# Merging the elementwise work of RWKV chunk steps over pairs and directions, with partition changes counted in the schedule

## The chip, the cores and the metric

The kernel runs on one core of a Trainium2 chip. The metric is the device time of one execution in microseconds (us): 3136.03 us, the median of 3 runs between 3131.77 and 3136.59. The profile is of a separate execution that took 3133.72 us; its span on the core is 3131.9 us. All numbers of the trace are from that one execution.

## What is computed

Two layers of a mixer over 640 tokens (128 context tokens, 512 latent ones) of width 2048. Every layer normalises and modulates its input, projects it with `w_in` to 7056 columns, runs three branches (gated linear attention with 6 heads, a chunked gMLP with 4 groups, bidirectional RWKV-7 with 12 heads), multiplies each by its gate and projects the result back with `w_out`. All matrix products of the projections are made in three parts of fp32r (a high and a low half of each factor). The change touches the RWKV branch, whose recurrence is, per head and direction,

```python
def step(s, inp):
    r_t, w_t, k_t, v_t, a_t, b_t = inp
    sa = jnp.einsum('bhvk,bhk->bhv', s, a_t)
    s = (s * w_t[:, :, None, :] + sa[..., None] * b_t[:, :, None, :]
         + v_t[..., None] * k_t[:, :, None, :])
    return s, jnp.einsum('bhvk,bhk->bhv', s, r_t)
```

The kernel runs it in chunks of 64 tokens: within a chunk everything is matrix products, and between chunks a 64x64 state per head and direction is handed on. With the state `s0`, the chunk's decay `p` per channel and the chunk's own contribution `Y`, both kernels compute the next state: before as `Y*p + s0*p`, after as `(Y + s0)*p`.

## The kernel before, in words

**The order is planned at build time.** Every operation is recorded by `rec` (line 134) and priced by `price` (line 215), and `run` (line 300) plays the program with one clock per engine. Each engine takes, of what is ready, the operation with the lowest priority number; the number is the place in the recording, less a boost for weights and for the RWKV chain. TensorE (`choose_pe`, line 363) prefers to go on with matrix products that use the whole array and collects small ones into groups. The order that comes out is fixed in the program: on the chip each engine takes its instructions in this order and waits for whichever is next. All instructions are issued from line 462, so the trace gives them that line, and they are told apart by their tiles. On VectorE an operation costs 0.066 us plus 0.00104 us per element (plus 0.062 us for a per-partition scalar); an operation that starts at another partition than the one before it costs nothing more. An engine's choice is made at line 402 for ScalarE and line 408 for the others.

**The RWKV branch** (`rwkv_quad`, line 895) works on a quad: two pairs of heads (`j`), both directions (`d`), five chunks. The two heads of a pair (`q`) lie in partitions 0 to 63 and 64 to 127. There are 12 quads (3 of each of 2 windows in 2 layers), one after the other, since they share the tiles `gb`, `ag`, `ken` and `svu`. A quad has a preparation (decays, the chunk matrices `ag`, `bk`, `gb`, and a 32x32 inversion on VectorE; from line 906 up to the steps) and then five chunk steps (the loop `for k in range(5)` from line 1075). A step is a chain:

1. ScalarE scales the eight states into `s0p` (`S.activation`, 64x64 each).
2. TensorE makes `X` and the first half of `Y` from `ag` and `svu`; VectorE copies `X` to `xs`.
3. TensorE adds `gb` times `xs`; VectorE copies the result back into `svu`, one copy for each direction and head (4 copies, 64x128).
4. TensorE adds the products with `ken` and `gb` to `Y`.
5. VectorE makes the next state, one `scalar_tensor_tensor` for each pair, direction and head (8 of 64x64), into `svu`, into `scar` (the state carried to the next window) or into `so` (the output state).

In the second window one direction hands no state on after the third step, and the other none after the fifth, so 432 of the 480 states (12 quads, 5 steps, 8 states) are made. The whole RWKV chain is boosted over everything but the weights. Between the chain's groups TensorE runs projections (`pz`), whose weights are split by ScalarE (`whi`) and VectorE (`wlo`), the other two branches and the modulation of the next layer (`mod_slow`, line 667; gangs of eight 128x32 products of 256 columns, priced at 0.111 us each). After the last quad `rwkv_end` (line 1194) finishes the branch and `out_proj` (line 1447) follows, which needs all branches.

Of the kernel before, what the change touches and what calls it, by code (L numbers as in the profile page):

```python
# [7 lines left out]
F32 = mybir.dt.float32  # L8
# [23 lines left out]


BOOST = 100000
RSTEP = 1
GANG = True
NRAW, NHI, NLO, N6 = 5,3,3,6
# [34 lines left out]

class _Op:
    __slots__ = ("idx", "eng", "fn", "args", "kw", "cost", "tail", "mode", "work", "lock", "succ", "npred", "ready", "prio",
                 "tiles", "first", "start", "end", "tab", "alts", "gang")


class Scheduler:
# [55 lines left out]
    def rec(self, eng, fn, args, kw):  # L134
        o = _Op()
        o.idx, o.eng, o.fn, o.args, o.kw = len(self.ops), eng, fn, args, kw
        o.succ, o.npred, o.ready, o.start, o.end = [], 0, 0.0, None, None
        o.prio = o.idx - self.boost
        wr, rd = [], []
        for i, a in enumerate(args):  # L140
            if hasattr(a, "tensor"):
                (wr if i == 0 else rd).append(a)
        for k, a in kw.items():
            if hasattr(a, "tensor"):
                (wr if k in ("out", "accum_out") else rd).append(a)
        self.price(o, eng, fn, wr, rd, kw)
        o.alts = None
        preds = {}
        names = set()
        rr = [r for r in map(self.region, rd) if r]  # L150
        ww = [r for r in map(self.region, wr) if r]
        for n, p0, p1, m in rr:
            names.add(n)
            for q0, q1, x, w in self.W.get(n, ()):
                if q0 < p1 and p0 < q1 and x & m:
                    preds[w] = 1
            if n in self.psum:
                for q0, q1, x, w in self.R.get(n, ()):
                    if self.ops[w].eng != eng:
                        preds[w] = 1  # L160
        for n, p0, p1, m in ww:
            names.add(n)
            for L, kind in ((self.W, 1), (self.R, 2)):
                keep = []
                for e in L.get(n, ()):
                    q0, q1, x, w = e
                    if q0 < p1 and p0 < q1 and x & m:
                        preds[w] = max(preds.get(w, 0), kind) if preds.get(w) != 1 else 1
                        if p0 <= q0 and q1 <= p1 and not (x & ~m):
                            continue  # L170
                    keep.append(e)
                L[n] = keep
        for n, p0, p1, m in rr:
            self.R.setdefault(n, []).append((p0, p1, m, o.idx))
        for n, p0, p1, m in ww:
            self.W.setdefault(n, []).append((p0, p1, m, o.idx))
        for n in names:
            preds.setdefault(self.head.setdefault(n, o.idx), 3)
        preds.pop(o.idx, None)
        o.gang = self.gang if eng == "PE" else None  # L180
        if o.gang is not None:
            for w in list(preds):
                if self.ops[w].gang is o.gang:
                    del preds[w]
            o.gang.append(o)
        for w, kind in preds.items():
            self.ops[w].succ.append((o.idx, kind))
        o.npred = len(preds)
        o.tiles = tuple(names)
        o.first = []  # L190
        for n in names:
            if n not in self.users:
                self.users[n] = 0
                t = self.tag[n]
                if t is not None:
                    self.seen.setdefault(t, []).append(n)
                    o.first.append(n)
            self.users[n] += 1
        self.ops.append(o)
        return o  # L200
# [14 lines left out]
    def price(self, o, eng, fn, wr, rd, kw):  # L215
# [9 lines left out]
        if eng == "PE":  # L225
            o.tail = 0.29
            if fn == "transpose":
                o.cost, o.work = 0.11, 0.053
                return
            l, r = kw["lhsT"], kw["rhs"]  # L230
            K, M, N = int(l.shape[0]), free(l), free(r)
            fast = l.dtype == F32R
            s = N / (2400 if fast else 600)
            o.work = s * K * M / 16384
            if (K == 128 or K * M == 0) and (M == 128 or (fast and M == 16)):
                o.cost = max(s + 0.0145, 0.107) if fast else max(s + 0.02, 0.15)
                return
            o.mode = f"{int(fast)} {K} {M}"
            if fast:
                o.cost = s + 0.0145  # L240
            elif M <= 32:
                o.cost = 0.03 if K <= 32 else 0.111 * N / 256
            elif M == 64:
                o.cost = (0.056 if K == 128 else 0.05) * max(N, 64) / 64
            else:
                o.cost = 0.55 if K == 16 else 0.206 * max(N, 100) / 128
            return
# [52 lines left out]
    def run(self):  # L300
# [11 lines left out]
        rel = {}  # L312
        order, dma, table, sw, mode = [], 0.0, None, 0, "full"
        window, work, fast = 0, 0.0, True
        left = dict(self.users)
        self.turns = 0

# [62 lines left out]
        while True:  # L380
# [15 lines left out]
            if e == "PE" and mode != "full" and all(ops[x[1]].mode == "full" for x in a):  # L396

                near = [x for x in f if x[0] < s + LINGER and ops[x[1]].mode != "full"]
                if near:
                    t[e] = min(near)[0]  # L400
                    continue
            if e == "ACT":

                i = take(a, min(range(len(a)), key=lambda j: (a[j][0] + (TABW if ops[a[j][1]].tab not in (None, table) else 0))))
            elif e == "PE":
                i = choose_pe(a, s)
            else:
                i = heapq.heappop(a)[1]
            o = ops[i]
            for n, o in enumerate(o.gang or [o]):  # L410
# [12 lines left out]
                elif o.tab is not None and o.tab != table:  # L423
                    x = 1.3
                    table = o.tab
                    sw += 1
                if o.lock:
                    s = free_at(e, True) if t[e] >= s else max(s, free_at(e, True))
                    locked[e] = s + c
# [64 lines left out]
def tile_hybrid(ctx: ExitStack, tc: tile.TileContext, I, O, layers=DEPTH, pairs=6, gpairs=3, cms=4, dbg=None):  # L494
# [71 lines left out]
    csp = cst.tile([128, KT, 32], F32, name="csp")  # L566
    modt = [cst.tile([128, 48, 2], F32, name=f"modt{l}") for l in range(layers)]
    amul = cst.tile([128, KT, 2], F32, name="amul")
    scar = [[cst.tile([128, 64], F32, name=f"scar{j}{d}") for d in range(2)] for j in range(2)]

    xr_d = dr.tile([NT, D], F32, name="xr_d")
    gate_d = [dr.tile([2, D], F32, name=f"gate_d{l}") for l in range(layers)]
# [318 lines left out]
    def product(out, a, b):  # L891
        f = dict(out=out, in0=a, in1=b, op=ALU.mult)
        V.tensor_tensor(**f)

    def rwkv_quad(l, P, wp, sts):

        ps2 = (2 * P, 2 * P + 1)
# [159 lines left out]
        for j, p in enumerate(ps2):  # L1057
            for d in range(2):
                for k, kind in start[d].items():
# [10 lines left out]
                            S.copy(out=svu[hq[q], j, d, q, pos(d, k), :], in_=ps[hq[q], 0:64])  # L1070
                    else:
                        for q in range(2):
                            S.copy(out=svu[hq[q], j, d, q, pos(d, k), :], in_=scar[j][d][hq[q], :])
        four = [(d, j, q) for d in range(2) for j in range(2) for q in range(2)]
        for k in range(5):
            X, Y = (PL().rearrange("p (a j d t) -> p a j d t", j=2, d=2, t=64) for _ in range(2))
            goes = [end[d].get(k, "next") for d in range(2)]
            s0p = ts2.tile([128, 2, 2, 64], F32, tag="s0p", name="s0p")
            sc = lambda d, j, q: p5[hq[q], 10 * j + 5 * d + pos(d, k):10 * j + 5 * d + pos(d, k) + 1]
            for d, j, q in four:  # L1080
                if goes[d]:
                    S.activation(out=s0p[hq[q], j, d], in_=svu[hq[q], j, d, q, pos(d, k), :], func=AF.Copy, scale=sc(d, j, q))
            with together():
                for d, j, q in four:
                    mm(X[hq[q], 0, j, d], ags[d][:, j, q, pos(d, k), 0:64], svu[:, j, d, q, pos(d, k), :], start=(d == 0 and j == 0))
# [4 lines left out]
            with together():  # L1090
                for d, j, q in four:
                    mm(X[hq[q], 1, j, d], gb[hq[q], j, d, pos(d, k), 0:64], xs[hq[q], j, d], start=False)
            for d in range(2):
                for q in range(2):
                    V.tensor_copy(out=svu[hq[q], :, d, q, pos(d, k), :], in_=X[hq[q], 1, :, d])
            with together():
                for d, j, q in four:
                    if goes[d]:
                        mm(Y[hq[q], 0, j, d], kens[d][:, j, q, pos(d, k), :], svu[:, j, d, q, pos(d, k), :], start=False)
                for d, j, q in four:  # L1100
                    mm(Y[hq[q], 1, j, d], gb[hq[q], j, d, pos(d, k), 64:128], svu[hq[q], j, d, q, pos(d, k), :], start=False)
            for j, p in enumerate(ps2):
                for d in range(2):
                    if not goes[d]:
                        continue
                    so = TS() if goes[d] == "out" else None
                    for q in range(2):
                        dst = svu[hq[q], j, d, q, pos(d, k + 1), :] if goes[d] == "next" else scar[j][d][hq[q], :] if goes[d] == "carry" else so[hq[q], :]
                        V.scalar_tensor_tensor(out=dst, in0=Y[hq[q], 0, j, d], scalar=sc(d, j, q), in1=s0p[hq[q], j, d], op0=ALU.mult, op1=ALU.add)
                    if so is not None:  # L1110
                        ps = PL()
                        for q in range(2):
                            mm(ps[hq[q], 0:64], so[hq[q], :], ident[hq[q], hq[q]])
                        s2 = TS()
                        S.copy(out=s2, in_=ps[:, 0:64])
                        Q.dma_start(out=O["new_rwkv"][0, l, d, 2 * p:2 * p + 2].rearrange("h v k -> (h v) k"), in_=s2)
# [573 lines left out]
```

## Time and profile before

| | before |
|---|---|
| median of 3 runs | 3136.03 us |
| profiled execution, its time / its span | 3133.72 / 3131.9 us |
| TensorE matmuls busy | 2898.4 us (93%) |
| VectorE busy | 2150.3 us (69%), 5200 instructions |
| ScalarE busy | 1197.9 us (38%), 2641 instructions |
| mean granted TensorE clock | 0.974 |

A busy TensorE is not one at its peak, since matrix products overlap in the pipeline; what counts is where it stands idle, and what ended that idle time. The stretch from 300 to 1350 us holds the quads of the first layer, that from 1640 to 2850 us those of the second; each is followed by the output projection.

### The profile page before, as it was taken

To read this page: it belongs to the slowest core of one execution; us is meant where nothing else is said; L and a number is where in the kernel's file an instruction comes from. 1 tells how busy PE (TensorE), PEld (TensorE's weight loads), DVE (VectorE), ACT (ScalarE), POOL (GpSimd) and SP (SyncE) were. 2 spreads that over 40 slices of the span, in tenths; PEclk is the share of its full clock that TensorE was granted. 3 is DMA by queue.
4 is the path that set the end of the run, shared out by engine and by line. 5 is a ranking of instruction groups with operands and counts; after the bars stand their busy time and mean duration, and the time that the engine had idled before them with its cause. 6 is when DMAs were issued, how large, how long until landed. Compare 5 with 4: busy or idle time off the path is not lost. (4 is left out here: it accounts for less than half of the span.)

```text
span 3131.9 us, 64037 instructions
## 1 busy us (share of the span) xinstructions
PE 2898.4 (93%) x24531; PEld 2559.2 (82%) x24531; DVE 2150.3 (69%) x5200; ACT 1197.9 (38%) x2641; POOL 105.0 (3%) x281
## 2 busy tenths in 40 slices
PE   4899999999899999999999999999989998998998
PEld 2688688788888878988879877888879887998786
DVE  3357686785776867655576668769778696866557
ACT  3252643435343354431015336344534335434001
POOL 0000000000000000000000000000000000000000
PEclk9899899999999999999999999999999999999999
DMA  9856375565555645465463654635534453437335
GB/s 307 261 157 170 92 203 142 160 182 155 148 142 161 182 118 150 124 206 161 125 201 104 176 140 139 186 95 137 156 98 121 107 155 96 103 99 228 114 111 194
DMA packets 672154, 478.13 MB, mean 153 GB/s; under 512 B 188596, under 2 KB 606088, under 8 KB 671848
## 3 DMA queue, kind: packets, MB, share of 16 engines
q1 hardware_dynamic: 671848, 474.04, 53.3%
q8 instruction: 194, 3.18, 0.4%
q14 instruction: 112, 0.92, 0.1%
HBM read 393.63 MB, written 79.59 MB: 151 GB/s over the span
## 5 line engine op out<-in xcount | busy, mean ns | idle before, releaser
L462 PE MATMUL pz<-hi,whi 128*128 128x320 f32 (+1 forms) x3504 | 902.2, 320 | 21.4 <-ACT t L462 14.3
L462 PE MATMUL pz<-lo,whi 128*128 128x320 f32 (+1 forms) x3504 | 890.2, 316 | 0.0
L462 PE MATMUL pz<-hi,wlo 128*128 128x320 f32 (+1 forms) x3504 | 881.2, 316 | 1.6 <-DVE wlo L462 1.6
L462 PEld LDWEIGHTS pz<-hi,whi 128*128 128x128 f32 (+1 forms) x3504 | 602.9, 189 | 50.2 <-ACT t L462 19.4
L462 PEld LDWEIGHTS pz<-lo,whi 128*128 128x128 f32 (+1 forms) x3504 | 602.7, 188 | 16.6 <-issue 7.2
L462 PEld LDWEIGHTS pz<-hi,wlo 128*128 128x128 f32 (+1 forms) x3504 | 600.1, 188 | 16.8 <-issue 6.9
L462 DVE TENSOR_TENSOR wlo<-raw,whi 128x512 fp32r<-128x512 f32 (+1 forms) x640 | 435.4, 681 | 223.8 <-ACT whi L462 198.5
L462 ACT ACTIVATE whi<-raw 128x512 fp32r<-128x512 f32 (+1 forms) x445 | 277.2, 623 | 770.6 <-PE pz L462 513.1
L462 PE MATMUL pl<-ag,bk 128*128 128x128 f32 x960 | 137.7, 291 | 48.7 <-DVE bk L462 33.5
L462 DVE CAST whi<-raw 128x512 fp32r<-128x512 f32 x195 | 81.8, 421 | 141.9 <-PE pz L462 56.8
L462 PEld LDWEIGHTS pl<-ag,bk 128*128 128x128 f32 x960 | 120.6, 198 | 70.4 <-issue 59.5
L462 ACT ACT_TABLE_LOAD x124 | 159.1, 1283 | 13.5 <-DMA t<-gl 8.9
L462 ACT ACTIVATE s0p<-svu,tsm 64x64 f32<-64x64 f32 x432 | 148.0, 345 | 5.8 <-POOL svu L462 0.3
L462 DVE TENSOR_TENSOR svu<-lk,svu 104x31 f32<-104x31 f32 (+15 forms) x372 | 125.9, 339 | 18.8 <-DMA lk<-nsc 11.6
L462 DVE TENSOR_TENSOR svu<-svu 104x31 f32<-104x31 f32 (+15 forms) x372 | 126.1, 339 | 7.4
L462 DVE SCALAR_TENSOR_TENSOR svu<-pl,tsm,s0p 64x64 f32<-64x64 f32 x336 | 95.1, 283 | 41.8 <-PE pl L462 33.5
L462 ACT ACTIVATE tw<-tw 128x320 f32<-128x320 f32 (+1 forms) x180 | 76.4, 448 | 108.6 <-DVE tw L462 104.8
L462 PE MATMUL pz<-whi,hi 128*128 128x512 f32 x288 | 113.3, 394 | 1.6 <-DVE whi L462 1.5
L462 PE MATMUL pz<-wlo,hi 128*128 128x512 f32 x288 | 111.9, 393 | 2.6 <-DVE wlo L462 2.5
L462 PE MATMUL pz<-whi,lo 128*128 128x512 f32 x288 | 112.2, 391 | 0.0
L462 DVE TENSOR_TENSOR ag<-win,tw 64x320 f32<-64x320 f32 x192 | 89.3, 483 | 29.3 <-DMA yd<-ag 13.8
L462 DVE TENSOR_TENSOR gb<-pl,kc 64x384 f32<-64x384 f32 x192 | 93.0, 484 | 22.7 <-PE pl L462 20.8
(241 smaller groups left out, 4119.9 us busy)
## 6 DMA issues: line engine op xcount, KB each, us to landing
raw<-in_w_in SPq DMA_DIRECT2D x440, 256.0 KB
raw<-in_w_mod SPq DMA_DIRECT2D x256, 256.0 KB
raw<-in_w_out SPq DMA_DIRECT2D x192, 256.0 KB
win<-kr SPq DMA_DIRECT2D x48, 480.0 KB
mraw<-in_w_mod SPq DMA_DIRECT2D x85, 256.0 KB
kr<-t SPq DMA_DIRECT2D x36, 320.0 KB
t<-od SPq DMA_DIRECT2D x32, 320.0 KB
vg<-t SPq DMA_DIRECT2D x24, 320.0 KB
```

What stands on the lines that cost most here:

```text
L462: getattr(self.real[o.eng], o.fn)(*o.args, **o.kw)
```

## The change

It edits the chunk step in three places, and the planner in three:

- `s0p` is a plain copy of the state, for both pairs and both directions at once (2 copies of 64x256, one for each head), with `at_pos` making the access pattern, since the two directions stand at mirrored chunks.
- the copies back into `svu` are 2 of 64x256 instead of 4 of 64x128.
- the next state is an addition over all 128 partitions (128x256), and then a product with the decays, which are read as a broadcast: 2 of 64x256 where both directions go on to the next chunk, 1 of 128x256 where both are carried; where the directions differ, each has its own.
- the planner notes the first partition of each output on VectorE and ScalarE. If it differs from that of the operation before, the start is held until 0.115 us (0.12 us on ScalarE) after that one's issue time.
- both engines choose, among the ready operations within 24 priority places of the first, one that starts at the partition of the operation before.
- a matrix product with up to 32 output partitions is priced at 0.16 us per 256 columns, not 0.111 us.

```diff
+DRAIN = {"DVE": 0.115, "ACT": 0.12}
+NEAR = 24
...
         self.price(o, eng, fn, wr, rd, kw)
+        (pitch, _), off = wr[0].ap[0], int(wr[0].offset)
+        o.part = off // int(pitch) if eng in DRAIN and pitch else 0
...
-                o.cost = 0.03 if K <= 32 else 0.111 * N / 256
+                o.cost = 0.03 if K <= 32 else 0.16 * N / 256
...
+        part, drain = dict.fromkeys(engs, 0), dict.fromkeys(engs, 0.0)
...
-            if e == "ACT":
+            if e in DRAIN:
 
-                i = take(a, min(range(len(a)), key=lambda j: (a[j][0] + (TABW if ops[a[j][1]].tab not in (None, table) else 0))))
+                p = a[0][0]
+                i = take(a, min(range(len(a)), key=lambda j: (a[j][0] > p + NEAR, ops[a[j][1]].part != part[e], a[j][0])))
...
+                if e in DRAIN:
+                    if o.part != part[e]:
+                        s = max(s, drain[e])
+                    part[e], drain[e] = o.part, s + x + c + DRAIN[e]
...
-    scar = [[cst.tile([128, 64], F32, name=f"scar{j}{d}") for d in range(2)] for j in range(2)]
+    scar = cst.tile([128, 2, 2, 64], F32, name="scar")
...
+    def at_pos(a, strides):
+
+        return bass.AP(tensor=a.tensor, offset=a.offset, ap=[a.ap[0]] + [[s, 2] for s in strides] + list(a.ap[1:]))
...
-            sc = lambda d, j, q: p5[hq[q], 10 * j + 5 * d + pos(d, k):10 * j + 5 * d + pos(d, k) + 1]
-            for d, j, q in four:
-                if goes[d]:
-                    S.activation(out=s0p[hq[q], j, d], in_=svu[hq[q], j, d, q, pos(d, k), :], func=AF.Copy, scale=sc(d, j, q))
+            for q in range(2):
+                if both:
+                    S.copy(out=s0p[hq[q]], in_=at_pos(svu[hq[q], 0, 0, q, pos(0, k), :], (1280, 640 + 64 * (4 - 2 * k))))
+                else:
+                    for d in range(2):
+                        if goes[d]:
+                            S.copy(out=s0p[hq[q], :, d], in_=svu[hq[q], :, d, q, pos(d, k), :])
...
-            for d in range(2):
-                for q in range(2):
-                    V.tensor_copy(out=svu[hq[q], :, d, q, pos(d, k), :], in_=X[hq[q], 1, :, d])
+            for q in range(2):
+                V.tensor_copy(out=at_pos(svu[hq[q], 0, 0, q, pos(0, k), :], (1280, 640 + 64 * (4 - 2 * k))), in_=X[hq[q], 1])
...
-                    for q in range(2):
-                        dst = svu[hq[q], j, d, q, pos(d, k + 1), :] if goes[d] == "next" else scar[j][d][hq[q], :] if goes[d] == "carry" else so[hq[q], :]
-                        V.scalar_tensor_tensor(out=dst, in0=Y[hq[q], 0, j, d], scalar=sc(d, j, q), in1=s0p[hq[q], j, d], op0=ALU.mult, op1=ALU.add)
...
+            if both:
+                V.tensor_tensor(out=s0p, in0=Y[:, 0], in1=s0p, op=ALU.add)
+                pk = lambda r: at_pos(p5[r, pos(0, k):pos(0, k) + 1].to_broadcast([r.stop - r.start, 64]), (10, 9 - 2 * k))
+                if goes[0] == goes[1] == "carry":
+                    V.tensor_tensor(out=scar, in0=s0p, in1=pk(slice(0, 128)), op=ALU.mult)
+                elif goes[0] == goes[1] == "next":
+                    for q in range(2):
+                        V.tensor_tensor(out=at_pos(svu[hq[q], 0, 0, q, pos(0, k + 1), :], (1280, 640 + 64 * (2 - 2 * k))),
+                                        in0=s0p[hq[q]], in1=pk(hq[q]), op=ALU.mult)
+            else:
+                for d in range(2):
+                    if goes[d]:
+                        V.tensor_tensor(out=s0p[:, :, d], in0=Y[:, 0, :, d], in1=s0p[:, :, d], op=ALU.add)
...
+                if goes[d] == "next":
+                    for q in range(2):
+                        V.tensor_tensor(out=svu[hq[q], :, d, q, pos(d, k + 1), :], in0=s0p[hq[q], :, d], in1=pj(hq[q]), op=ALU.mult)
+                elif goes[d] == "carry":
+                    V.tensor_tensor(out=scar[:, :, d], in0=s0p[:, :, d], in1=pj(slice(0, 128)), op=ALU.mult)
+                else:
+                    for j, p in enumerate(ps2):
+                        so = TS()
+                        V.tensor_scalar(out=so, in0=s0p[:, j, d], scalar1=p5[:, 10 * j + 5 * d + pos(d, k):10 * j + 5 * d + pos(d, k) + 1],
+                                        scalar2=None, op0=ALU.mult)
```

## Rows read from the trace of the kernel before

**Rows 1.** The page's part 1: busy us, share of the span, instructions.

```profile
PE 2898.4 (93%) x24531; PEld 2559.2 (82%) x24531; DVE 2150.3 (69%) x5200; ACT 1197.9 (38%) x2641; POOL 105.0 (3%) x281
```

**Rows 2.** Busy time by window; the first line names the columns.

```profile
core 0: us, PE busy (x) PEld busy (x) DVE busy (x) ACT busy (x) POOL busy (x), PEclk, DMA share, GB/s
300.00:1350.00 1050.00, 983.25 (x9591) 869.42 (x9589) 768.02 (x1937) 461.60 (x1035) 44.65 (x120) 0.97 0.54 149
1350.00:1400.00 50.00, 44.99 (x326) 43.02 (x325) 25.46 (x64) 17.49 (x37) 0.00 (x0) 0.97 0.81 247
1640.00:2850.00 1210.00, 1142.13 (x10546) 1044.94 (x10547) 883.22 (x2162) 539.00 (x1196) 51.63 (x134) 0.98 0.47 128
2850.00:2910.00 60.00, 46.81 (x256) 40.70 (x255) 43.08 (x106) 22.28 (x40) 0.00 (x0) 0.91 0.88 276
```

**Rows 3.** What TensorE's matmuls waited for, 300 to 2850 us: us, times, longest.

```profile
PE pl L462 <- DVE bk L462: 29.9, 26, 7.3
PE pl L462 <- DVE tw L462: 27.9, 29, 2.9
PE pl L462 <- DVE ag L462: 15.3, 22, 1.9
PE pz L462 <- ACT t L462: 14.1, 13, 2.6
PE pm L462 <- DVE ss L462: 9.0, 4, 4.3
PE pl L462 <- DVE xs L462: 1.6, 4, 0.7
PE pl L462 <- DVE svu L462: 0.7, 1, 0.7
```

**Rows 4.** A stall in a preparation, busy time by window, columns as in Rows 2.

```profile
2576.00:2591.00 15.00, 6.64 (x28) 3.62 (x27) 14.56 (x51) 4.07 (x7) 0.28 (x2) 0.60 0.35 99
```

**Rows 5.** Groups of instructions, the step's own: busy us, mean ns, idle before.

```profile
L462 ACT ACTIVATE s0p<-svu,tsm 64x64 f32<-64x64 f32 x432 | 148.0, 345 | 5.8 <-POOL svu L462 0.3
L462 DVE SCALAR_TENSOR_TENSOR svu<-pl,tsm,s0p 64x64 f32<-64x64 f32 x336 | 95.1, 283 | 41.8 <-PE pl L462 33.5
L462 DVE COPY svu<-pl 64x128 f32<-64x128 f32 x240 | 68.9, 287 | 54.9 <-PE pl L462 32.1 <-ACT s0p L462 7.4 <-ACT whi L462 5.5
```

**Rows 6.** Timeline, VectorE in chunk steps: start us, us, count, idle before.

```profile
333.89 2.45 DVE L462 SCALAR_TENSOR_TENSOR svu<-pl,tsm,s0p 64x64 f32<-64x64 f32 x8 [1.64 <-PE pl L462]
2836.05 1.25 DVE L462 COPY svu<-pl 64x128 f32<-64x128 f32 x4 [2.11 <-PE pl L462]
```

**Rows 7.** Groups of instructions nearest to the new forms, as in Rows 5.

```profile
L462 DVE TENSOR_TENSOR gb<-pl,kc 64x256 f32<-64x256 f32 x96 | 39.8, 415 | 1.6 <-PE pl L462 1.1
L462 DVE TENSOR_TENSOR md<-md,pm 128x256 f32<-128x256 f32 x32 | 13.4, 418 | 15.2 <-PE pm L462 14.9
L462 ACT COPY ss<-pm 64x256 f32<-64x256 f32 x48 | 17.6, 367 | 6.9 <-PE pm L462 6.3
L462 ACT COPY svu<-pl 64x64 f32<-64x64 f32 x48 | 9.9, 206 | 11.8 <-PE pl L462 11.1
L462 ACT COPY svu<-scar 64x64 f32<-64x64 f32 x48 | 11.1, 242 | 32.4 <-DVE svu L462 14.3 <-DMA wd<-svu 10.7 <-DVE scar L462 6.1
```

**Rows 8.** Timeline, VectorE operations that all start at partition 0, columns as in Rows 6.

```profile
2553.74 0.43 DVE L462 TENSOR_TENSOR tw<-tw,tw 128x256 f32<-128x256 f32 x1
2554.09 0.31 DVE L462 TENSOR_TENSOR svu<-lk,svu 104x156 f32<-104x156 f32 x1
2554.32 0.41 DVE L462 TENSOR_REDUCE tsm<-tw 128x4 f32<-128x256 f32 x1
```

**Rows 9.** Timeline, TensorE: one gang of the modulation (16 records), and what follows.

```profile
603.37 1.07 PE L462 MATMUL pm<-raw,csp 128*32 128x256 f32 x16
604.37 0.82 PE L462 MATMUL pl<-ag,bk 128*128 128x128 f32 x5
```

**Rows 10.** The first quad's chunk steps, busy time by window, columns as in Rows 2.

```profile
320.00:375.00 55.00, 51.39 (x534) 35.70 (x538) 31.93 (x76) 29.73 (x71) 0.00 (x0) 0.81 0.29 88
```

More of the change, by code (lines that the diff above doesn't have):

```diff
@@ L74 @@
     __slots__ = ("idx", "eng", "fn", "args", "kw", "cost", "tail", "mode", "work", "lock", "succ", "npred", "ready", "prio",
-                 "tiles", "first", "start", "end", "tab", "alts", "gang")
+                 "tiles", "first", "start", "end", "tab", "alts", "gang", "part")
 class Scheduler:
@@ L1072, in rwkv_quad @@
                         for q in range(2):
-                            S.copy(out=svu[hq[q], j, d, q, pos(d, k), :], in_=scar[j][d][hq[q], :])
+                            S.copy(out=svu[hq[q], j, d, q, pos(d, k), :], in_=scar[hq[q], j, d])
         four = [(d, j, q) for d in range(2) for j in range(2) for q in range(2)]
@@ L1077, in rwkv_quad @@
             goes = [end[d].get(k, "next") for d in range(2)]
+            both = all(goes)
             s0p = ts2.tile([128, 2, 2, 64], F32, tag="s0p", name="s0p")
-            sc = lambda d, j, q: p5[hq[q], 10 * j + 5 * d + pos(d, k):10 * j + 5 * d + pos(d, k) + 1]
-            for d, j, q in four:
-                if goes[d]:
-                    S.activation(out=s0p[hq[q], j, d], in_=svu[hq[q], j, d, q, pos(d, k), :], func=AF.Copy, scale=sc(d, j, q))
+            for q in range(2):
[5 more added lines that the diff above has]
+                            S.copy(out=s0p[hq[q], :, d], in_=svu[hq[q], :, d, q, pos(d, k), :])
             with together():
@@ L1101, in rwkv_quad @@
                     mm(Y[hq[q], 1, j, d], gb[hq[q], j, d, pos(d, k), 64:128], svu[hq[q], j, d, q, pos(d, k), :], start=False)
-            for j, p in enumerate(ps2):
-                for d in range(2):
-                    if not goes[d]:
-                        continue
-                    so = TS() if goes[d] == "out" else None
-                    for q in range(2):
-                        dst = svu[hq[q], j, d, q, pos(d, k + 1), :] if goes[d] == "next" else scar[j][d][hq[q], :] if goes[d] == "carry" else so[hq[q], :]
-                        V.scalar_tensor_tensor(out=dst, in0=Y[hq[q], 0, j, d], scalar=sc(d, j, q), in1=s0p[hq[q], j, d], op0=ALU.mult, op1=ALU.add)
-                    if so is not None:
+            if both:
[8 more added lines that the diff above has]
+            else:
+                for d in range(2):
+                    if goes[d]:
+                        V.tensor_tensor(out=s0p[:, :, d], in0=Y[:, 0, :, d], in1=s0p[:, :, d], op=ALU.add)
@@ new lines, in rwkv_quad @@
+            for d in range(2):
+                if not goes[d] or both and goes[0] == goes[1]:
+                    continue
+                pj = lambda r: at_pos(p5[r, 5 * d + pos(d, k):5 * d + pos(d, k) + 1].to_broadcast([r.stop - r.start, 64]), (10,))
+                if goes[d] == "next":
+                    for q in range(2):
+                        V.tensor_tensor(out=svu[hq[q], :, d, q, pos(d, k + 1), :], in0=s0p[hq[q], :, d], in1=pj(hq[q]), op=ALU.mult)
[6 more added lines that the diff above has]
+                                        scalar2=None, op0=ALU.mult)
```

## The prediction, made before the changed kernel was run

> **What bounds the kernel now.** The page's shares come first: TensorE is busy for 93% of the span, VectorE for 69%, ScalarE for 38% [rows 1]. So neither engine that the change relieves is the bound as a whole. The windows then show where TensorE is not busy [rows 2]. In the two stretches that hold the quads it stands idle for 1050 - 983.3 + 1210 - 1142.1 = 134.6 us; just behind them, where the branch is finished and the output projection is waited for, for 5.0 us (first layer) and 13.2 us (second). The waits of TensorE name who ends that idle time [rows 3]. The large entries are VectorE in the preparation of a quad (`bk`, `ag`, `tw`) and in linear attention (`ss`); what the chunk step makes on VectorE, `xs` and `svu`, is waited for for 1.6 and 0.7 us only, because the plan puts projections between the chain's groups. The entries shown that name VectorE come to 84.4 us, the one that names ScalarE to 14.1 us. A stretch of 15 us shows what such a wait looks like [rows 4]: VectorE is full (14.6 us), TensorE works for 6.6 us, and the granted clock is 0.60, a mix of full speed (2.4 GHz) and half (1.2 GHz).
>
> So three things can move the end: the length of the chain at the two layer ends, the waits on a full VectorE in the preparations, and the order.
>
> **Step 1, the chunk step's VectorE work.** Before: a state lasts 283 ns and a copy 287 ns [rows 5], but eight states in a row take 2.45 us and four copies 1.25 us, 306 and 313 ns each [rows 6]: 432 x 0.306 + 240 x 0.313 = 207 us. After, counted from the diff: 120 copies of 64x256, 48 additions of 128x256 and 12 of 128x128, 72 products of 64x256, 24 of 64x128, 6 of 128x256 and 24 scalings of 128x64. The nearest rows have 415 ns for a 64x256 operation that reads PSUM and a repeated mask, and 418 ns for a 128x256 one with one input in PSUM [rows 7]; a change of half adds some 0.03 us, as in rows 6. With 0.45 us for a 64x256, 0.42 us for a 128x256, 0.29 us for a 128x128 (as one of 64x128 [rows 5]) and 0.31 us for the smaller ones it is 54.0 + 20.2 + 3.5 + 32.4 + 7.4 + 2.5 + 7.4 = 127 us. VectorE loses 80 us. The product with a strided broadcast stands in no row; 0.29 us (64x128) and 0.56 us (as far above 0.42) are its bounds, and I take 0.42, that of the same shape: 72 x 0.14 = 10 us either way on VectorE.
>
> On the step's loop, where both directions go on, 2.45 + 1.25 = 3.70 us become 0.42 + 2 x 0.45 + 2 x 0.45 = 2.22 us. The chain is 1.48 us shorter per step, 89 us over 60 steps, 44 us per layer.
>
> What of it lies on the path? TensorE's work stays and hardly waits for this loop [rows 3]. A shorter chain lets the projections run later, behind the last quad, where TensorE is idle. The 13.2 and 5.0 us there [rows 2] are covered by work left over; with part of the finish still waiting for its transfers I take **-14 us** (bounds 0 and -18). If the projections ran out first, all 44 us of a layer would count; that is the first rival.
>
> **Step 2, ScalarE.** 432 scalings of 345 ns [rows 5], 0.36 us with the change of half, are 155 us. A 64x256 copy from PSUM takes 367 ns and a 64x64 one 206 from PSUM and 242 from SBUF [rows 7], so one from SBUF 0.40, with the change 0.42 us: 96 x 0.42 + 24 x 0.30 = 47 us. ScalarE loses 108 of the 1001 us it is busy in the two stretches, 11%. TensorE waits 14.1 us for projections that ScalarE evacuates (`t` [rows 3]); they stand behind a scaling only by chance. I take a third, **-5 us** (0 to -14).
>
> **Step 3, the waits on VectorE.** VectorE loses 80 of 1651 us in the two stretches [rows 2], 5%, but in the steps, not in the preparations where the waits are. There the planner acts. The trace bears its price out: three operations that all start at partition 0 begin 0.08 us before the one in front has ended [rows 8], while in the alternating states each begins 0.02 us after [rows 5, 6]. So a change of half costs about 0.1 us, and the old plan, which has 0.195 us for a state of 64x64, was 0.11 us short for each. Preparations alternate halves too (`ag`, `bk`, `gb`). An order with fewer changes saves VectorE time where it is full, and a plan that knows the rest no longer puts a matrix product ahead of a result that comes late. Bounds: 0, and -84 us if all the waits on VectorE went. Much of the preparation is the inversion, whose links each wait for the last and begin at partition 0 anyway, so I take a quarter: **-21 us**.
>
> The VectorE page of the Trainium skill (VectorE: DVE Perf Modes, section "The DRAIN you can't avoid") says that after every operation the next does not start until the pipeline is empty. By that, the order of halves would be worth nothing and step 3 would fall to about zero; it is the third rival. Rows 8 speak against it.
>
> **Step 4, the price of small products.** A gang takes 1.00 us from its first product to the next group [rows 9]; the plan had 8 x 0.111 = 0.89 us and now has 1.28. It is as wrong as before, the other way. Too high a price makes nothing wait by itself; I take 0 (between -3 and +10 us, the latter 0.15 us for each of the 64 gangs that the code makes of 32 groups).
>
> **The sum.** -14 - 5 - 21 = -40 us. The profiled execution took 3133.7 us, so 3093.7; the runs' median is 2.3 us above it, so **3096 us**. The forecast's own range is 3065 to 3122 us (each term between its half and its double, not all at once). A measurement of this kernel can tell 0.2% from no change, some 6 us.
>
> **Rivals.**
>
> - *The chain sets the end.* Then the whole 89 us of step 1 and 5 of step 2 come off: 3042 us. For it: quads stand one after the other over both stretches, and the second layer's idle 13.2 us lie behind the chain's end. Against it: projections are still running there, and TensorE is busy for 94% of the stretches [rows 2]. 12%.
> - *TensorE's work sets the end and the waits only move.* Work is unchanged, the new order has as many waits elsewhere: 3136 us, give or take 6. For it: `xs` and `svu` are hardly waited for [rows 3]. Against it: 84 us of idle with VectorE's name. 15%. This is also the case in which the planner's choice does not do what it says, because two operations of the same half are seldom ready together.
> - *Every operation drains*, the skill's rule: steps 1 and 2 alone, 3136 - 19 = 3117 us. 8%.
> - *Slower, by the clock.* In the first quad's steps, where few projections lie between the small products, the granted clock was 0.81 [rows 10], against 0.97 and 0.98 in the stretches [rows 2]. A shorter chain packs these groups closer in all twelve quads. Each 0.01 of the mean clock over 2260 us is 22.6 us of TensorE's work; from 0.02 lower the sum of 40 us is eaten. Twelve stages of 45 us at 0.81 would lower the mean by 0.04 (89 us); if the clock falls by three quarters of that, 0.03, it is 68 - 40 = +28 us: 3164 us. Against it: with the projections filling the gaps most quads keep the full clock now. 12%.
>
> **How the numbers follow.** The forecast keeps 53%. Faster by over 0.2%: 53 + 12 + 8 and 4 of the second rival, 77%. Within 0.2%: 7, slower: 4 + 12 = 16. The range 3048 to 3146 us takes in the forecast's own range, the drain case, the undecided case and the upper half of the chain's; it leaves out the slow clock and half of the chain's, 18%.
>
> **What the changed profile would show.** Steps 1 and 2: 120 copies into `svu` near 0.42 us and no `scalar_tensor_tensor` into it, VectorE's busy time near 2070 us, ScalarE's near 1090; chunk steps about 1.5 us closer together. Step 1's share: TensorE without the idle 13.2 us behind the second layer's quads. Step 3: fewer waits for `bk`, `ag`, `tw`, their sum on VectorE's name near 63 us. The forecast is wrong if those waits stay while the step shrinks (the second rival), if the mean clock falls under 0.96 (the fourth), or if the last quad ends 44 us earlier per layer and the output projection with it (the first).

## The result, and the profile after

The changed kernel takes 3091.14 us (median of 4 runs, 3083.25 to 3094.93) against 3134.84 us for the kernel before in the same session: a ratio of 0.9858, 95% interval 0.9836 to 0.9881. The forecast was 3096 us. Its profiled execution took 3083.25 us, with a span of 3081.5 us, 50.4 us less than before.

Part 1 of the page (busy us, share of the span, instructions):

```profile
PE 2854.2 (93%) x24531; PEld 2542.6 (83%) x24531; DVE 2068.5 (67%) x4837; ACT 1082.3 (35%) x2322; POOL 104.7 (3%) x281
```

Against [rows 1], VectorE lost 81.8 us and ScalarE 115.6 us. TensorE has as many instructions as before and 44.2 us less busy time, so only 50.4 - 44.2 = 6.2 us of the gain shows as less idle time. A matrix product of 320 columns is recorded with 0.31 us while the next starts 0.15 us behind it, as here in the kernel before:

```profile
337.43 0.31 PE L462 MATMUL pz<-hi,whi 128*128 128x320 f32 x1
337.58 0.31 PE L462 MATMUL pz<-lo,whi 128*128 128x320 f32 x1
337.73 0.31 PE L462 MATMUL pz<-hi,wlo 128*128 128x320 f32 x1
```

A wait shorter than the difference makes TensorE look busy. That the 44.2 us are such waits is the likeliest reading; no run tests it. The groups of the new forms answer to [rows 5, 7] (busy us, mean ns, idle before):

```profile
L472 DVE COPY svu<-pl 64x256 f32<-64x256 f32 x120 | 50.6, 421 | 62.2 <-PE pl L472 59.8
L472 ACT COPY s0p<-svu 64x256 f32<-64x256 f32 x96 | 38.6, 402 | 11.1 <-DVE svu L472 9.4 <-DVE tsm L472 0.4
L472 DVE TENSOR_TENSOR svu<-s0p,tsm 64x256 f32<-64x256 f32 x72 | 30.2, 419 | 2.0
L472 DVE TENSOR_TENSOR s0p<-pl,s0p 128x256 f32<-128x256 f32 x48 | 20.4, 425 | 46.7 <-PE pl L472 46.4
```

The timeline of one step's VectorE work (start us, us, count, idle before) answers to [rows 6]:

```profile
2777.69 0.88 DVE L472 COPY svu<-pl 64x256 f32<-64x256 f32 x2 [0.49 <-PE pl L472]
...
2780.52 0.42 DVE L472 TENSOR_TENSOR s0p<-pl,s0p 128x256 f32<-128x256 f32 x1 [1.96 <-PE pl L472]
2780.98 0.87 DVE L472 TENSOR_TENSOR svu<-s0p,tsm 64x256 f32<-64x256 f32 x2
```

3.70 us on the loop have become 0.88 + 0.42 + 0.87 = 2.17 us. The busy time by window (columns as in [rows 2], the stretches set to the new ends of the quads, those behind the quads as long as in [rows 2]):

```profile
300.00:1320.00 1020.00, 958.36 (x9611) 859.61 (x9611) 727.07 (x1757) 404.07 (x877) 45.14 (x120) 0.98 0.55 153
1320.00:1370.00 50.00, 43.23 (x297) 41.54 (x294) 24.17 (x62) 16.20 (x36) 0.00 (x0) 0.97 0.87 255
1640.00:2795.00 1155.00, 1097.90 (x10388) 1015.13 (x10387) 823.21 (x1948) 474.36 (x1014) 45.83 (x126) 0.98 0.48 132
2795.00:2855.00 60.00, 40.45 (x203) 33.64 (x202) 39.21 (x95) 19.43 (x37) 0.00 (x0) 0.80 0.82 265
```

TensorE's idle time in the two stretches is 61.6 + 57.1 = 118.7 us (134.6 before), the clock in them is what it was. Behind the quads it idles longer than before, for 6.8 and 19.6 us (5.0 and 13.2 before), and the clock in the last stretch is 0.80 (0.91 before). What TensorE waited for, 300 to 2810 us, answers to [rows 3]:

```profile
PE pl L472 <- DVE tw L472: 36.7, 28, 6.4
PE pl L472 <- DVE bk L472: 19.6, 18, 3.8
PE pl L472 <- DVE gb L472: 11.4, 18, 1.6
...
PE pm L472 <- DVE ss L472: 9.4, 3, 4.4
...
PE pz L472 <- ACT t L472: 6.9, 6, 1.9
```

The wait for `bk` is a third shorter and that for `ag` is gone, but `tw` has grown and `gb` is new. [rows 3] and these lines are a choice from each list. All entries that name VectorE come to 104.1 us before and to 104.4 us here, those that name ScalarE to 27.6 and 13.0 us. So the waits on VectorE by name do not account for the gain. The timeline shows where the time went. The copies to `xs` mark the chunk steps; here are the first and the last of each layer, in the timeline of the kernel before:

```profile
328.49 0.42 DVE L462 COPY xs<-pl 128x256 f32<-128x256 f32 x1 [0.22 <-PE pl L462]
...
1347.73 0.42 DVE L462 COPY xs<-pl 128x256 f32<-128x256 f32 x1
...
1864.92 0.42 DVE L462 COPY xs<-pl 128x256 f32<-128x256 f32 x1 [0.22 <-PE pl L462]
...
2833.51 0.42 DVE L462 COPY xs<-pl 128x256 f32<-128x256 f32 x1
```

and of the changed kernel:

```profile
328.82 0.42 DVE L472 COPY xs<-pl 128x256 f32<-128x256 f32 x1 [0.36 <-PE pl L472]
...
1313.08 0.42 DVE L472 COPY xs<-pl 128x256 f32<-128x256 f32 x1
...
1828.14 0.42 DVE L472 COPY xs<-pl 128x256 f32<-128x256 f32 x1 [0.22 <-PE pl L472]
...
2783.35 0.42 DVE L472 COPY xs<-pl 128x256 f32<-128x256 f32 x1 [0.36 <-PE pl L472]
```

The first layer's quads take 984.3 us and not 1019.2 (-35.0), the way to the second layer 515.1 and not 517.2 (-2.1), its quads 955.2 and not 968.6 (-13.4); from the last step to the end it is 298.1 and 298.4 us. The quads' shorter time is 48.4 of the 50.4 us. Within the quads, the 48 distances between neighbouring steps add up to 435.4 us (488.9 before, -53.5), and the preparations between the quads to 1504.1 us (1498.9 before).

That reading gave two theories for the experiments. **A:** the length of the chain sets the end, nearly in full. **B:** the forecast's sum, with the step worth 19 us (14 by the chain, 5 by ScalarE) and the planner 21. Theory C (the planner alone) and D (the load on VectorE, wherever it lies) are further rivals.

### The profile page after: what moved, and what is told of

Read it like the earlier page. It is cut to its first block, busy times and chain, and to the rows that moved or that the text cites. A ratio compares the mean times of both kernels' runs of the same rounds, so it can differ in the third digit from the quotient of the medians.

```text
span 3081.5 us, 63374 instructions
## 1 busy us (share of the span) xinstructions
PE 2854.2 (93%) x24531; PEld 2542.6 (83%) x24531; DVE 2068.5 (67%) x4837; ACT 1082.3 (35%) x2322; POOL 104.7 (3%) x281
## 5 line engine op out<-in xcount | busy, mean ns | idle before, releaser
L472 PE MATMUL pl<-ag,bk 128*128 128x128 f32 x960 | 130.7, 283 | 33.3 <-DVE bk L472 20.6
L472 DVE TENSOR_TENSOR ag<-pl,kc 64x384 f32<-64x384 f32 x192 | 89.6, 484 | 6.3 <-PE pl L472 5.0
L472 DVE COPY svu<-pl 64x256 f32<-64x256 f32 x120 | 50.6, 421 | 62.2 <-PE pl L472 59.8
```

The costliest lines, as they stand in the source:

```text
L472: getattr(self.real[o.eng], o.fn)(*o.args, **o.kw)
```

## The experiments

Ratios are to the kernel before in the same session.

### The merged steps alone

```diff
-            if e in DRAIN:
+            if e == "ACT":
...
-                if e in DRAIN:
-                    if o.part != part[e]:
-                        s = max(s, drain[e])
-                    part[e], drain[e] = o.part, s + x + c + DRAIN[e]
...
-                o.cost = 0.03 if K <= 32 else 0.16 * N / 256
+                o.cost = 0.03 if K <= 32 else 0.111 * N / 256
```

> The merged chunk step with the planner of before: no partition held or preferred, 0.111 us for small products. Theory A (the length of the chain of chunk steps sets the end: the distances between steps fell by 53.5 us in all and the span by 50.4): nearly all of the gain is here, 3091 us, give or take 8. Theory B (the forecast's sum: the step is worth 19 us, the planner 21): 3116 us. Theory C (the planner alone does it): 3135 us.

Measured: 3113.27 us, ratio 0.9909 (0.9892 to 0.9927), 28.6 us less than before. Between A and B; by this one order the planner has a share.

### The planner alone

The planner's hunks of the change on the kernel before; the chunk step is that of before.

> The chunk step of before with all three edits of the planner. Theory A: 3135 us, give or take 8. Theory B: 3114 us, and TensorE waits some 20 us less on VectorE in the preparations. Theory C: 3091 us.

Measured: 3133.7 us, ratio 0.9972 (0.9961 to 0.9983), 8.8 us less. C falls, and B with its 3114 us: TensorE's waits that name VectorE (300 to 2850 us) went from 104.1 to 94.9 us, not down by 20. VectorE's busy time went from 2150.3 to 2110.0 us with the steps of before, so the plan does save VectorE time, but little of it came off the whole.

### Without the preference for the same partition

```diff
-                i = take(a, min(range(len(a)), key=lambda j: (a[j][0] > p + NEAR, ops[a[j][1]].part != part[e], a[j][0])))
+                i = take(a, min(range(len(a)), key=lambda j: (a[j][0] + (TABW if ops[a[j][1]].tab not in (None, table) else 0))))
```

> The changed kernel without the preference for the same first partition; the price of a change of partition and that of small products stay. Theory A: 3091 us, give or take 8. Theory B, if the preference is what saves VectorE time: 3105 to 3112 us; if the price is: 3091 us.

Measured: 3093.67 us, ratio 0.9856 (0.9824 to 0.9888), as the changed kernel. The preference is worth nothing that this can tell.

### The old price of small products

```diff
-                o.cost = 0.03 if K <= 32 else 0.16 * N / 256
+                o.cost = 0.03 if K <= 32 else 0.111 * N / 256
```

> The changed kernel with small products priced at 0.111 us per 256 columns again. Theories A and B: 3091 us, give or take 8, since a price makes nothing wait by itself. If the higher price costs something, as the measured 1.00 us for a gang would have it, up to 10 us less: 3081 us.

Measured: 3079.86 us, ratio 0.9809 (0.9790 to 0.9827), 15 us better than the changed kernel by the ratios. That is outside what A and B gave, and beyond the 10 us of the third expectation, in the direction that it named.

### A longer chain

```diff
                 V.tensor_tensor(out=s0p, in0=Y[:, 0], in1=s0p, op=ALU.add)
+                for _ in range(3):
+                    V.tensor_tensor(out=s0p, in0=s0p, in1=s0p, op=ALU.max)
```

> The changed kernel with three more VectorE operations of 128x256 behind the addition of the states in 48 of the 60 steps, each waiting for the last (the maximum of the sum with itself, so no value changes): about 1.3 us more on the loop of a step, 62 us on the chain, and 60 us more VectorE work. Theory A (the chain's length sets the end): 50 to 60 us slower than the changed kernel, so as slow as before, a ratio of about 1.000 to 1.004. Theory D (what counts is how much of TensorE's time is lost to many short waits on a busy VectorE and ScalarE, and the chain's length only through them): 15 to 30 us slower, ratio 0.991 to 0.996, and like the next run.

Measured: 3143.66 us, ratio 1.0007 (0.9992 to 1.0021), 0.0149 or 47 us above the changed kernel. The timeline shows the three operations on the loop:

```profile
2832.36 0.42 DVE L472 TENSOR_TENSOR s0p<-pl,s0p 128x256 f32<-128x256 f32 x1 [2.27 <-PE pl L472]
2832.82 1.34 DVE L472 TENSOR_TENSOR s0p<-s0p 128x256 f32<-128x256 f32 x3
2834.20 0.87 DVE L472 TENSOR_TENSOR svu<-s0p,tsm 64x256 f32<-64x256 f32 x2
```

and the window at the second layer's end shows what a late chain does there, TensorE busy for 40 of 70 us at a clock of 0.67, because the projections have run out before the last quad is done:

```profile
2800.00:2870.00 70.00, 40.02 (x583) 32.02 (x581) 32.90 (x79) 16.97 (x43) 1.20 (x2) 0.67 0.31 82
```

The mean granted clock of the profiled execution is 0.964, against 0.975 in the changed kernel; how much of the 47 us is the lower clock, no run separates.

### The same work off the chain

```diff
                                         in0=s0p[hq[q]], in1=pk(hq[q]), op=ALU.mult)
+                for _ in range(3):
+                    V.tensor_tensor(out=s0p, in0=s0p, in1=s0p, op=ALU.max)
```

> The same three operations in the same 48 steps, but on the sum after the next state has been made from it, so that the next step does not wait for them: the same 60 us more VectorE work, nothing on the loop. Theory A: the changed kernel's time within 8 us, ratio 0.984 to 0.989. Theory D: like the run before, 15 to 30 us slower, ratio 0.991 to 0.996.

Measured: 3102.95 us, ratio 0.9877 (0.9851 to 0.9904), 6 us above the changed kernel by the ratios. In the timeline the three stand behind the products that make the next state; the copy to `xs` starts 1.45 us after the end of the products in this step, and 1.50 us after it in the step of the changed kernel that the section on the result shows, without such operations:

```profile
2787.32 0.87 DVE L472 TENSOR_TENSOR svu<-s0p,tsm 64x256 f32<-64x256 f32 x2
2788.22 1.34 DVE L472 TENSOR_TENSOR s0p<-s0p 128x256 f32<-128x256 f32 x3
2789.64 0.42 DVE L472 COPY xs<-pl 128x256 f32<-128x256 f32 x1
```

Not all 48 stand beside the chain. In the second step of a quad of the first window one direction's state goes out and the other's goes on; there the code makes the products after the three operations. These are 6 of the 48 steps, with 1.3 us each on the chain, 8 us in all:

```profile
339.41 0.42 DVE L472 TENSOR_TENSOR s0p<-pl,s0p 128x256 f32<-128x256 f32 x1 [0.67 <-PE pl L472]
339.87 1.34 DVE L472 TENSOR_TENSOR s0p<-s0p 128x256 f32<-128x256 f32 x3
341.58 0.60 DVE L472 TENSOR_TENSOR svu<-s0p,tsm 64x128 f32<-64x128 f32 x2
```

The same instructions, 41 us apart by where they stand, with one order for each: D falls. VectorE's busy time is 2126.1 and 2119.3 us in the two, so the load alone does not do it.

### Chance in the order

```diff
-DRAIN = {"DVE": 0.115, "ACT": 0.12}
+DRAIN = {"DVE": 0.11, "ACT": 0.115}
```

> The changed kernel with the price of a change of first partition at 0.110 and 0.115 us instead of 0.115 and 0.120. Nothing real changes but the order that the planner happens to find, so what this differs from the changed kernel is how far chance in the order goes. All theories: ratio 0.982 to 0.990. If it is further off, single differences of 15 us between kernels here mean little.

Measured: 3110.71 us, ratio 0.9900 (0.9875 to 0.9925), 13 us above the changed kernel. An edit that changes nothing but the order that the planner finds is worth that much, so no two kernels here can be told apart by 15 us, and each part needs more than one order.

### The price of a change of partition alone

The merged steps and that price; no preference, small products at 0.111 us (the edits of the third and the fourth experiment together).

> The merged steps with the price of a change of first partition alone: no preference for the same partition, small products at 0.111 us. The run without the preference had 0.986 and the one with the old price of small products 0.981. If the price of the change is what the planner's part is worth, and the preference nothing, and the higher price of small products costs 14 us: 0.981. If the preference helps and its absence was made up by something else: 0.986 to 0.991, as with the merged steps alone.

Measured: 3073.02 us, ratio 0.9783 (0.9754 to 0.9812), the fastest of all. TensorE's waits for `bk`, 300 to 2850 us, are here

```profile
PE pl L471 <- DVE bk L471: 5.6, 6, 1.5
```

and in the merged steps alone, which differ by this price only, they are as follows; the second orders below do not bear this difference out:

```profile
PE pl L467 <- DVE bk L467: 25.1, 25, 2.1
```

### Second orders for three of them

Each has the same nudge of the planner:

```diff
-SLK = 0.3
+SLK = 0.29
```

The kernel before:

> The kernel before with one allowance of its planner (for the start of a matrix product behind another engine's result) at 0.29 instead of 0.30 us: only the order changes. Chance moved the changed kernel by 13 us in the run before. If chance is as large here: 0.996 to 1.005. If the order of before was a lucky or an unlucky one, this leaves that range, and part of the gain is chance.

Measured: 3158.68 us, ratio 1.0069 (1.0054 to 1.0084). Of these two orders, that of before was the lucky one.

The merged steps alone:

> The merged steps with the planner of before, nudged in the same way. The first try gave 0.991. If the price of a change of partition has no worth of its own and 0.991 was an unlucky order: 0.980 to 0.988, as the four kernels with that price. If the merged steps alone are worth some 30 us: 0.987 to 0.995.

Measured: 3095.77 us, ratio 0.9866 (0.9851 to 0.9881), 13 us better than the first order and in the range given for an unlucky first one; but it is still above both orders with the price of a change. That speaks for a worth of its own; the nearest two of the four are 0.0065 or 20 us apart, about as much as the nudge moved the kernel before.

The price of a change alone:

> The merged steps with the price of a change of partition alone (the kernel that had 0.978), nudged in the same way. If its lead over the changed kernel is real: 0.974 to 0.983. If it was chance: 0.983 to 0.990.

Measured: 3077.14 us, ratio 0.9801 (0.9781 to 0.9821). The lead over the changed kernel stands. The waits do not explain it. In the second orders those for `bk` and `tw`, 300 to 2850 us, are with the price

```profile
PE pl L471 <- DVE tw L471: 50.3, 31, 7.3
PE pl L471 <- DVE bk L471: 18.5, 9, 8.2
```

and without it

```profile
PE pl L467 <- DVE tw L467: 34.8, 26, 6.4
PE pl L467 <- DVE bk L467: 23.6, 21, 2.6
```

All waits that name VectorE come to 89.6 and 110.6 us in the two orders with the price, and to 108.3 and 108.7 us in the two without.

### The copies on two engines

```diff
-                V.tensor_copy(out=at_pos(svu[hq[q], 0, 0, q, pos(0, k), :], (1280, 640 + 64 * (4 - 2 * k))), in_=X[hq[q], 1])
+                (S.copy if q else V.tensor_copy)(out=at_pos(svu[hq[q], 0, 0, q, pos(0, k), :], (1280, 640 + 64 * (4 - 2 * k))), in_=X[hq[q], 1])
```

> The kernel that had 0.978, with the copy of the second head's result in the step on ScalarE, so that the two copies run side by side: about 0.42 us less on the loop of a step, 25 us over 60 steps, 26 us less work for VectorE and 24 us more for ScalarE. Theory A (the longer chain cost 45 us for 62): about 18 us faster than that kernel, 0.972, give or take chance (0.004). Theory D: ScalarE's load takes back what VectorE gives, 0.978, give or take chance.

Measured: 3097.91 us, ratio 0.9877 (0.9857 to 0.9897), some 27 us above the two orders of the kernel that it starts from. A miss, and the timeline says why the premise did not hold. VectorE's copy of one step:

```profile
2778.50 0.42 DVE L471 COPY svu<-pl 64x256 f32<-64x256 f32 x1 [0.30 <-PE pl L471]
```

and ScalarE's of the same step:

```profile
2779.01 0.37 ACT L471 COPY svu<-pl 64x256 f32<-64x256 f32 x1 [1.97 <-DVE svu L471]
```

The second starts 0.51 us behind the first, released by it: the recorder makes a read of a PSUM tile wait for an earlier read of the same tile by another engine. The loop got no shorter (0.51 + 0.37 = 0.88 us, as with two copies on VectorE), and the sum of the distances between steps is 458.1 us, not 452.0 or 446.4. Why it is slower is not shown; ScalarE's queue now holds a link of the chain, and 27 us is more than chance moved the others by.

### All orders side by side

The ratios, with the sum of the 48 distances between steps, that of the 10 preparations between the quads of a layer, the way from the first layer's last step to the second layer's first, and the time from the last step to the end; all are added up from the `xs` copies of each profiled execution, in us:

| kernel | ratio | 48 distances | preparations | layer to layer | last step to end |
|---|---|---|---|---|---|
| before / its second order | 1 / 1.0069 | 488.9 / 478.0 | 1498.9 / 1523.3 | 517.2 / 547.7 | 298.4 / 282.2 |
| planner alone | 0.9972 | 486.4 | 1520.1 | 515.6 | 279.7 |
| merged steps alone / second order | 0.9909 / 0.9866 | 458.9 / 457.2 | 1479.5 / 1464.9 | 546.5 / 529.8 | 301.4 / 314.0 |
| with price of a change / second order | 0.9783 / 0.9801 | 452.0 / 446.4 | 1473.7 / 1487.6 | 518.6 / 518.0 | 299.7 / 301.5 |
| with that and the preference | 0.9809 | 445.6 | 1503.7 | 511.6 | 285.9 |
| the change / nudged | 0.9858 / 0.9900 | 435.4 / 454.0 | 1504.1 / 1504.4 | 515.1 / 544.1 | 298.1 / 281.3 |
| the change without the preference | 0.9856 | 458.1 | 1459.9 | 541.0 | 303.4 |
| longer chain / same work off it | 1.0007 / 0.9877 | 502.9 / 460.1 | 1515.2 / 1518.7 | 511.0 / 512.7 | 279.8 / 286.4 |
| price of a change, copies on two engines | 0.9877 | 458.1 | 1505.9 | 515.6 | 286.4 |

From means over the orders: merged steps 0.9888 against 1, or against the 1.0035 of the two orders of before: **-35 to -46 us**. Price of a change: 0.9888 to 0.9792, **-30 us**. Preference: 0.9792 to 0.9809, +5 us, within chance. Higher price of small products: 0.9798 (three kernels without it) to 0.9871 (three with it), **+23 us**. Together -37 to -48 us; the changed kernel and its nudged order had -45 and -31. With two or three orders for each part, and 6 to 22 us between two orders of one kernel, these are sizes and not measurements to a few us.

The columns say where the orders differ. The way from layer to layer takes 511 to 519 us in nine of the kernels and 530 to 548 in five, and a nudge can move a kernel from one kind to the other: of the three nudges that moved the time by 13 us or more, two changed this way by 29 and 31 us, the third by 17. The price of a change shortens this way by 20 us in the means and the preparations not at all (1472 us without, 1481 with). Why some orders take the long way is open. The time from the last step to the end tells whether projections were left over. Here are the 60 us behind the last step of the nudged change (281.3 us to the end) and of the second order of the merged steps (314.0 us), columns as in [rows 2]:

```profile
2830.12:2890.12 60.00, 25.54 (x144) 17.80 (x139) 28.81 (x83) 7.80 (x23) 0.00 (x0) 0.66 0.67 202
2778.02:2838.02 60.00, 54.17 (x396) 51.71 (x391) 30.61 (x78) 17.63 (x39) 0.00 (x0) 0.97 0.77 228
```

TensorE is busy for 25.5 us in the one, at a clock of 0.66, and for 54.2 us in the other, at 0.97.

## Why the prediction was right, and where it was right by luck

**Step 1's counts and durations held.** VectorE 2068.5 us (said: near 2070), the strided broadcast product 419 ns (taken: 0.42 us between 0.29 and 0.56), the loop 2.17 us (said 2.22).

**Its share on the path was mis-sized, and its way was wrong.** I let 14 of 89 us count: the idle time behind the last quads, which projections left over would fill. That idle time did not go. In stretches of equal length it was 5.0 and 13.2 us, and is 6.8 and 19.6 us now. What got shorter are the quads. That TensorE does not wait by name for the loop only says that the planner puts other work there; it does not say that the chain may be long. The length of the chain does count, as one pair of orders shows: 62 us more on it cost 47 us, the same work in 42 of the 48 steps beside it 6 us, and the sums of the distances differ by 42.8 us. But that pair makes the chain longer, until the projections run out before the last step. In the kernel before and in the changed kernel projections were still left behind the last step (298 us to the end, against 280 where none were), so for a shorter chain it is an argument and not a measurement. In the means of two orders the merged steps alone have 25 us less in the distances, but also 39 us less in the preparations, for a gain of 35 to 46 us. How much of the gain is the chain, and how much the 82 us less work on VectorE, is open; 60 us of work beside the chain cost only 6 us, which speaks for the chain.

The rival "the chain sets the end" looked at the right thing, and its price was too high: the loop lost 1.5 us, but a step's distance only 1.1 us in the changed kernel (53.5 over 48) and 0.7 us in the mean of all orders of the merged step without added work (451 against 483). The rest is waiting between the groups of a step, which no run here divides further.

**Step 2** (ScalarE, -5 us) was not tried by itself. ScalarE lost 115.6 us (said 108), and TensorE's wait for its `t` fell from 14.1 to 6.9 us, as forecast in direction; what that is worth in the whole is not shown.

**Step 3 was right in size (-21, measured -30), and not in its way.** The price in the plan is what counts, and the preference for the same half is worth nothing that these runs can tell. The 21 us were to come from shorter waits on VectorE in the preparations, 84 us down to 63. The three that it named, `bk`, `tw` and `ag`, fell from 73.1 to 56.3 us, but others grew, and all entries that name VectorE came to 104.1 us before and to 104.4 us after. Of the two orders with the price alone one waits less than the two without it (89.6 us against 108.3 and 108.7) and one does not (110.6 us), and both are faster. So the right size is luck: the 30 us come off elsewhere, by place mostly between the layers, and the cause is open.

The rule of the Trainium skill (VectorE: DVE Perf Modes, "The DRAIN you can't avoid"), as the prediction read it, gave this step about zero. The prediction took half of it: the same paragraph adds that an operation which is not held starts earlier, and points to the section "Two Vector instructions with no wait between them". By that one, an instruction is held until all earlier ones have finished if its partitions start in another quadrant (group of 32 partitions) than those last used. The trace agrees: where halves alternate, eight states of 283 ns take 2.45 us, so each starts (2.45 - 0.28) / 7 = 0.31 us after the one in front and 0.03 us behind its end; where all start at partition 0, the next starts 0.08 us before the end [rows 5, 6, 8]. So the rival "every operation drains" falls by these rows; the 30 us for a plan that knows which operations overlap speak against it too.

**Step 4 was wrong.** I called the new price of a gang as wrong as the old; against the 1.00 us measured [rows 9], 1.28 is 0.28 too high and 0.89 was 0.11 too low. And I gave it 0, at most +10 us; six kernels have it at +23, with no overlap between the three with and the three without. The nearest two are 15 us apart, which chance alone can make, so the sign is likely and the size rough. That a price makes nothing wait is true of the instructions, not of the plan. Which places in the order it spoils is open.

So 3096 us against 3091 is luck, from errors that cancel: the step is worth some 35 to 46 us, not 19, the price of a change 30, not 21, and the small products' price costs some 23, not 0. The slow-clock rival did not happen: the clock was 0.975, and 0.974 before.

The kernel that the experiments point to is the merged step with the price of a change alone: 0.9783 and 0.9801 in its two orders, some 20 us faster than the change as it stands.

## What to carry to other kernels

Where a long chain is woven into filling work, a wait that names the chain's tiles may be almost absent and the chain's length may still count: lay the first and the last link of each stage side by side, and test by putting the same work once on the chain and once beside it. Where a planner fixes the order, nudge one of its numbers to see how far chance goes (here 6 to 22 us) before a difference is put down to an edit, and compare idle time in stretches of equal length and waits by their whole sum, not by the entries that the edit was meant for. Take a price into a plan only if the trace has it: 0.16 us for products that take 0.125 each did worse than 0.111 in three orders against three.

## What the runs showed of the hardware

A change of first partition costs about 0.1 us on VectorE (0.03 us behind the end instead of 0.08 us before it [rows 5, 6, 8]), and the plan gained some 30 us, in the means of two orders each, from knowing it. TensorE's "busy" time fell by 44.2 us with the same 24531 instructions at the same mean clock, 0.975 and 0.974; waits shorter than the recorded length of a matrix product can stand in it. A product with a broadcast strided over pairs and directions took 419 ns for 64x256, and a copy from PSUM into mirrored places 421 ns, so the repeated and the mirrored access pattern cost no more than some 6 ns beside the nearest forms (415 and 418 ns [rows 7]).
